# RWKV-7 beside sparse attention on one core: the first unit's finish, join and chain run as a stream beside the second unit's preparation, at rank offset 1000

## The chip, the cores and the metric

The kernel runs on one core of a Trainium2 chip. The metric is the device time of one execution in microseconds (us); the profile's times count from the start of the profiled execution.

## The reference: what is computed

One layer of a streaming encoder over 1024 new prompt frames and 32 frames of a running stream. One input projection feeds two head groups, whose outputs are concatenated, projected and followed by an MLP:

```
group A: indexer scores -> the top min(256, L // 4) keys of a query -> softmax attention over those keys
group B (RWKV-7), 8 heads of 64, a matrix state S per head, frame by frame:
    r, k, v, decay, a, g = projections of the token-shifted row
    S = S * diag(decay) + (S @ (-kk)) (kk * a)^T + v k^T
    y = S @ r ; then a norm per head, a bonus term and the gate g
out = x + [attention, rwkv] @ w_out ;  out = out + relu(norm(out) @ w1)^2 @ w2
```

## The kernel before: how the work is staged and ordered

**Stages.** From 0 to about 450 us the kernel projects, scores and makes the masks of the chosen keys. From there to 924 us two generators are interleaved by `body`: `attn_all` goes through the attention items (pairs of a key head and a tile of 128 queries), and `rwkv_all` through RWKV. The output projection follows (936 to 990), then the MLP (990 to 1802).

**An attention item** is `query` (transpose L1135, scalings L1138 on ACT and L1139 on DVE, which make the tile Q), `scores` (matmuls L1151 and L1152, masked on DVE at L1154, exponential on ACT at L1157), `turn` (transposes L1175, copied out at L1176) and `product` (matmuls L1191, transpose L1195, then L1197 to L1199). The masks themselves (`mb`) are finished on DVE and ACT at L387 to L405; the last of them are still being made when the first items run.

**RWKV** works in five units: four of 256 prompt frames, each in four chunks of 64, and one of 32 sample frames. The chunk form solves a triangular system per chunk, with these pieces:

- `rwkv_front` prepares a unit: low-rank projections L629, statistics L793, scans L650, broadcast L809, the tile KB at L684, and per chunk the matrix G (matmuls L715, masked at L718). It ends with the first part of `lane_inverse`, mostly on POOL.
- `finish` (the inner function of `lane_inverse`): 64 matmuls L856 (128 records in the trace), DVE L857, 64 matmuls L862, DVE L866 (4) and the transposes L871 (2).
- `rwkv_join`: matmuls L771, copies L774 on ACT, matmuls L779, copies L782.
- `rwkv_tokens`: transposes L749 and L753 for one chunk.
- `rwkv_back`, the chain, for each chunk: R (L906, and L910 with the state `st`), U (L918, copied out at L919 and L920), the new state S (L925) and the output Y (L936, L940). Each needs the one before, and the state goes from chunk to chunk and unit to unit.
- `rwkv_norm`: L978 to L1003.

**What sets the order.** The program is written out by the generators; then a scheduler gives each engine one fixed list by the ranks of the instructions. `S.tc.high_priority(n)` ranks what is written inside it n instructions earlier. The chain has BOFF = 300, the front of unit 0 F0 = 200, all others 0. Each engine then runs its list strictly in order. For the steps around the change `rwkv_all` (L1012 to L1077) decides: in its pass `i` it takes turns between the chain of unit `i`, the norm of unit `i - 1` and the front of unit `i + 2`. In pass -1, beside the front of unit 1, the generator `first` writes unit 0's tokens for two chunks, waits JOIN0 = 4 turns, writes `finish`, waits two turns and writes the join; unit 0's chain is begun in pass 0. For the later units `rwkv_back` itself writes the next unit's `finish` and join behind its own chunks. KB of unit 1 lies in the same memory as the last masks' working tile, so L684 of unit 1 waits for the mask work.

Of the kernel before, what the change touches and what calls it, by code (L numbers as in the profile page):

```python
# [79 lines left out]
def keys_of(t):  # L80
    return 128 * (t + 1) if t < 8 else 544
# [70 lines left out]
def phase_a(S, pwx, pwy, pa, pi, px, xp, ps, late):  # L152
# [102 lines left out]

    def key_T(A, B, col, src, r):
        pt = ps.tile([128, 512], F32, name="pt", bufs=2)
        nc.tensor.transpose(pt[:, :r], flat(src), S.ident[:r, :r])
        nc.scalar.copy(A[:, col:col + r], pt[:, :r])
        nc.vector.tensor_tensor(B[:, col:col + r], pt[:, :r], A[:, col:col + r].bitcast(F32), op=ALU.subtract)  # L260

# [40 lines left out]
    def idx_tile(t, W):  # L302
# [14 lines left out]
        n = keys_of(t)  # L317
        A, B = (ksA, ksB) if t == 8 else (kiA, kiB)
        for h in range(8):
            w = iw[:r, t, h:h + 1]  # L320
            rl = late["pj"].tile([128, 1024], F32, name="rl", bufs=2)
            for c0 in range(0, n, 512):
# [3 lines left out]
                nc.tensor.matmul(o, qs[:, h // 2, h % 2, :r], A[:, c0:c1], start=True, stop=False)  # L326
                nc.tensor.matmul(o, qs[:, h // 2, h % 2, :r], B[:, c0:c1], start=False, stop=True)
                nc.scalar.activation(rl[:r, c0:c1], o, AF.Relu)
# [269 lines left out]

def rwkv_front(S, u, U, B):

# [74 lines left out]
    yield  # L675
    while B and B.tokens < B.NC:
        yield
# [50 lines left out]
def rwkv_prelude(S, rp, U):  # L728
    nc = S.nc
    n, t0 = U.n, U.t0  # L730
    U.v = v = rp.tile([128, 4, 256], F32, name="v", bufs=2)[:, :, :n]
    nc.sync.dma_start(v, S.zsd[1024:1536, t0:t0 + n].rearrange("(h p) t -> p h t", p=128))
    U.zg = zg = rp.tile([96, 256], F32, name="zg", bufs=2)
    nc.sync.dma_start(zg[:, :n], S.zsd[1600:1696, t0:t0 + n])
    nc.scalar.activation(zg[:, :n], zg[:, :n], AF.Tanh, scale=0.5)
    nc.vector.tensor_scalar(zg[:, :n], zg[:, :n], 0.5, 0.5, op0=ALU.mult, op1=ALU.add)


def rwkv_tokens(S, rp, ps, U, c):

    nc, w = S.nc, U.w
    KBs = rp.tile([128, 2, 4, 64], F32, name="KBs", bufs=TOKB)
    VU = rp.tile([128, 2, 4, 64], F32, name="VU", bufs=TOKB)
    if w < 64:
        nc.gpsimd.memset(VU, 0.0)
    for par in range(2):
        p = ps.tile([128, 4, 64], F32, name=TOKP[0], bufs=TOKP[1])
        for hp in range(4):
            nc.tensor.transpose(p[:, hp], U.KB[PAR[par], c, hp].rearrange("p a b -> p (a b)"), S.ident[PAR[par], PAR[par]])  # L749
        nc.scalar.copy(KBs[:, par], p)  # L750
    p = ps.tile([64, 4, 2, 64], F32, name=TOKP[0], bufs=TOKP[1])
    for hp in range(4):
        nc.tensor.transpose(p[:w, hp].rearrange("p a b -> p (a b)"), U.v[:, hp, c * w:c * w + w], S.ident)  # L753
    for par in range(2):
        nc.scalar.copy(VU[par * 64:par * 64 + w, par], p[:w, :, par])
    U.tokens = c + 1
    return KBs, VU


def rwkv_join(S, ps, U):  # L760

    nc = S.nc
    X1 = U.X1.rearrange("p (c h) t -> p c h t", c=4)

    def pc():
        return ps.tile([128, 512], F32, name="pr", bufs=PRB).rearrange("p (a b c) -> p a b c", a=4, b=4)
    p = pc()
    for cc in range(4):
        for hp in range(4):
            for par, b in ((0, 64), (1, 0)):  # L770
                nc.tensor.matmul(p[b + 32:b + 64, cc, hp], U.G[b:b + 32, par, cc, hp, 32:64], X1[b:b + 32, cc, hp],  # L771
                                 start=True, stop=True)
    for par, b in ((0, 64), (1, 0)):
        nc.scalar.copy(X1[b + 32:b + 64], p[b + 32:b + 64])  # L774
    p = pc()
    for cc in range(4):
        for hp in range(4):
            for par, b in ((0, 64), (1, 0)):
                nc.tensor.matmul(p[b:b + 32, cc, hp], X1[b + 32:b + 64, cc, hp], U.G[b + 32:b + 64, par, cc, hp, 32:64],  # L779
                                 start=True, stop=True)  # L780
    for par, b in ((0, 64), (1, 0)):
        nc.scalar.copy(U.G[b:b + 32, par, :, :, 32:64], p[b:b + 32])  # L782
# [190 lines left out]
def rwkv_norm(S, rp, ps, U):  # L973

    nc = S.nc
    n, y = U.n, U.y
    for g, p in head_bcast(S, ps, U.bst, n):
        nc.vector.tensor_tensor(U.v[:, 2 * g:2 * g + 2], U.v[:, 2 * g:2 * g + 2], p, op=ALU.mult)  # L978
    yf = y.rearrange("p h c t -> p h (c t)")[:, :, :n]
    sq = S.rs.tile([128, 4, 256], F32, name="tmp", bufs=2)[:, :, :n]  # L980
    for g in range(2):
        p = ps.tile([128, 2, 256], F32, name="pr", bufs=PRB)[:, :, :n]
        for h in range(2):
            nc.tensor.matmul(p[:, h], S.cen, yf[:, 2 * g + h], start=True, stop=True)
        nc.scalar.activation(sq[:, 2 * g:2 * g + 2], p, AF.Square)
        nc.vector.tensor_copy(yf[:, 2 * g:2 * g + 2], p)
    yield
    rn = head_stat(S, ps, sq, n)
    nc.vector.tensor_scalar(rn, rn, 1.0 / 64, 64e-5, op0=ALU.mult, op1=ALU.add)
    rsqrt_small(S, rn, rn, rn.shape[1])  # L990
    yield
    for g, p in head_bcast(S, ps, rn, n):
        for h in range(2):
            hp = 2 * g + h
            nc.vector.scalar_tensor_tensor(yf[:, hp], yf[:, hp], S.pv[:, 64 + hp:65 + hp], p[:, h], op0=ALU.mult, op1=ALU.mult)
            nc.vector.scalar_tensor_tensor(yf[:, hp], yf[:, hp], S.pv[:, 68 + hp:69 + hp], U.v[:, hp], op0=ALU.add, op1=ALU.add)
    yield
    for g in range(2):
        p = ps.tile([128, 2, 256], F32, name="pr", bufs=PRB)[:, :, :n]
        for h in range(2):  # L1000
            hp = 2 * g + h
            nc.tensor.matmul(p[:, h], S.g2[:, hp * 128:hp * 128 + 128], U.zg[:, :n], start=True, stop=True)
        nc.vector.tensor_tensor(yf[:, 2 * g:2 * g + 2], yf[:, 2 * g:2 * g + 2], p, op=ALU.mult)  # L1003
    nc.sync.dma_start(S.od[512:1024, U.t0:U.t0 + n].rearrange("(h p) t -> p h t", p=128), yf)
    yield


YB = 2
JOIN0 = 4


def rwkv_all(S, order):  # L1012

    state = {"st": None}
    S.units = units = [K() for _ in order]
    fronts = []
    for i, U in enumerate(units):
        U.i, U.stage, U.tok = i, 0, []
        U.next = units[i + 1] if i + 1 < len(units) else None
        fronts.append(rwkv_front(S, order[i], U, units[i - 2] if i > 1 else None))  # L1020

    def ahead(i):

        for _ in fronts[i]:
            if units[i].stage == 2 and i + 1 < len(order) and PRE and i >= PREI:
                break
            yield
        else:
            return
        yield  # L1030
        for _ in range(PRE):
            next(fronts[i + 1])
            yield
        yield from fronts[i]

    def norm(i):
        if i >= 0:
            yield from rwkv_norm(S, S.P[0], S.ps, units[i])
        if 0 <= i + 2 < len(order):
            rwkv_prelude(S, S.P[0], units[i + 2])  # L1040

    def first():

        U = units[0]
        for c in range(2):
            U.tok.append(rwkv_tokens(S, S.P[0], S.ps, U, c))
            yield
        for _ in range(JOIN0):
            yield
        U.finish()  # L1050
        for _ in range(2):
            yield
        rwkv_join(S, S.ps, U)
        yield

    for i in range(-2, len(order) + 1):
        gens = []
        B = front = None
        if 0 <= i < len(order):
            B = units[i]  # L1060
            gens.append(back := rwkv_back(S, S.P[0], S.ps, B, state))
        if i >= -1:
            gens.append(norm(i - 1))
            if i == -1:
                gens.append(first())
            if i == 0:
                shift_rows(S, S.P[0], S.ps)
        if i + 2 < len(order):
            gens.append(front := ahead(i + 2))
        while gens:  # L1070
            for g in list(gens):
                with S.tc.high_priority(BOFF) if B and g is back else S.tc.high_priority(F0 if i == -2 else F1 if i == -1 else FOFF) if g is front else nullcontext():
                    if next(g, 1) == 1:
                        gens.remove(g)
                yield
# [338 lines left out]
F0 = 200  # L1414
F1 = 0
# [15 lines left out]
BOFF = 300  # L1431
TOKB = 3
FOFF = 0
# [156 lines left out]
```

## Time and profile before

| | us |
|---|---|
| runs of the kernel | 1806.84, 1811.15, 1806.84 (median 1806.84) |
| the profiled execution, time / span | 1804.16 / 1802.4 |
| PE busy in the span | 1683.8 (93%) |
| DVE, ACT, POOL busy | 915.8, 711.5, 530.5 |
| stretch 485 to 593 us: PE busy | 88.31 of 108 |
| stretch 593 to 924 us: PE busy | 313.71 of 331 |

The span is what the profiler's records cover; 1.76 us of the execution lie outside it. [...]

### The profile page before, as it was taken

To read this page: it belongs to the slowest core of one execution; us is meant where nothing else is said; L and a number is where in the kernel's file an instruction comes from. 1 tells how busy PE (TensorE), PEld (TensorE's weight loads), DVE (VectorE), ACT (ScalarE), POOL (GpSimd) and SP (SyncE) were. 2 spreads that over 40 slices of the span, in tenths; PEclk is the share of its full clock that TensorE was granted. 3 is DMA by queue.
4 is the path that set the end of the run, shared out by engine and by line. 5 is a ranking of instruction groups with operands and counts; after the bars stand their busy time and mean duration, and the time that the engine had idled before them with its cause. 6 is when DMAs were issued, how large, how long until landed. Compare 5 with 4: busy or idle time off the path is not lost.

```text
span 1802.4 us, 32468 instructions
## 1 busy us (share of the span) xinstructions
PE 1683.8 (93%) x12966; PEld 1525.7 (85%) x12966; DVE 915.8 (51%) x2016; ACT 711.5 (39%) x1559; POOL 530.5 (29%) x759
## 2 busy tenths in 40 slices
PE   7999979986688998999989999999999999999999
PEld 6787769986465877777668789999999999999998
DVE  6476899975876686664552632222222222222224
ACT  5365667897544453443631332222212121212120
POOL 6568863353312131122120022222212222222120
PEclk9999989996686797996989999999999999999999
DMA  7211131323100102020333341111111111111105
GB/s 213 58 35 43 42 87 61 111 70 87 32 27 18 38 21 59 25 96 15 90 91 108 123 125 47 47 48 36 53 41 53 41 51 44 47 40 55 36 17 170
DMA packets 161087, 112.77 MB, mean 63 GB/s; under 512 B 31632, under 2 KB 150120, under 8 KB 160936
## 3 DMA queue, kind: packets, MB, share of 16 engines
q1 hardware_dynamic: 152104, 106.37, 20.2%
q10 hardware_dynamic: 8832, 4.33, 0.9%
q8 instruction: 102, 1.67, 0.4%
q14 instruction: 49, 0.40, 0.1%
HBM read 85.65 MB, written 25.01 MB: 61 GB/s over the span
## 4 chain that ended last, share of the span: by engine, by line
PE 51%; DMA 1%; ACT 1%; DVE 1%; issue 0%; SPq 0%; POOL 0%; DVEq 0%; ACTq 0%
PE pd L1372 20%; PE pr L1392 10%; PE pc L1392 5%; PE po L1392 5%; PE pd L1308 3%; PE pr L1308 2%; PE po L1191 1%; PE ptr L1175 0%; PE ptr L1406 0%; DMA of<-od 0%; PE ptr L145 0%; PE pc L925 0%; DMA w1r<-in_w_ff_dram 0%; PE pr L749 0%; ACT G L1274 0%
## 5 line engine op out<-in xcount | busy, mean ns | idle before, releaser
L1372 PE MATMUL pd<-hh,w1h 128*128 128x352 f32 x768 | 248.6, 324 | 2.3 <-issue 1.5
L1372 PE MATMUL pd<-hh,w1l 128*128 128x352 f32 x768 | 248.2, 323 | 0.7 <-DVE w1l L1239 0.7
L1372 PE MATMUL pd<-hl,w1h 128*128 128x352 f32 x768 | 247.5, 322 | 0.0
L1378 DVE TENSOR_TENSOR h2l<-rl,h2h 128x352 fp32r<-128x352 f32 x96 | 56.8, 592 | 277.7 <-ACT h2h L1377 277.7
L1238 ACT CAST w2h<-w2r 128x512 fp32r<-128x512 f32 x64 | 39.8, 621 | 293.3 <-PE po L1392 144.7
L1376 POOL TENSOR_TENSOR rl<-rl 128x352 f32<-128x352 f32 x96 | 85.2, 888 | 215.6 <-ACT rl L1375 215.6
L1372 PEld LDWEIGHTS pd<-hh,w1h 128*128 128x128 f32 x768 | 144.7, 188 | 2.8 <-issue 1.7
L1372 PEld LDWEIGHTS pd<-hh,w1l 128*128 128x128 f32 x768 | 144.8, 189 | 0.9 <-DVE w1l L1239 0.9
L1372 PEld LDWEIGHTS pd<-hl,w1h 128*128 128x128 f32 x768 | 145.3, 189 | 0.0
L1239 POOL TENSOR_TENSOR w2l<-w2r,w2h 128x512 fp32r<-128x512 f32 x32 | 41.6, 1299 | 299.2 <-ACT w2h L1238 288.7
L1392 PE MATMUL pr<-h2h,w2l 128*128 128x352 f32 x384 | 124.3, 324 | 0.0
L1392 PE MATMUL pr<-h2h,w2h 128*128 128x352 f32 x384 | 124.3, 324 | 0.0
L1392 PE MATMUL pr<-h2l,w2h 128*128 128x352 f32 x384 | 124.2, 323 | 0.0
L363 ACT ACTIVATE AR<-G,cnd 128x768 bf16<-128x768 f32 (+2 forms) x93 | 96.8, 1041 | 42.8 <-DVE cnd L368 35.2
L1375 ACT ACTIVATE rl<-pd 128x352 f32<-128x352 f32 x96 | 44.3, 463 | 143.5 <-PE pd L1372 137.0
L1398 DVE TENSOR_TENSOR ya<-ya,pr 128x352 f32<-128x352 f32 x84 | 43.8, 521 | 100.7 <-PE pr L1392 100.7
L1175 PE MATMUL ptr<-ident,s 128*128 128x128 f32 (+2 forms) x328 | 67.8, 309 | 21.1 <-DVE Kl L1120 13.2
L1157 ACT ACTIVATE s<-s,m 32x544 f32<-32x544 f32 (+8 forms) x72 | 55.5, 771 | 64.1 <-DVE m L1154 62.4
L1377 ACT CAST h2h<-rl 128x352 fp32r<-128x352 f32 x96 | 46.6, 485 | 75.7 <-POOL rl L1376 75.7
L1392 PEld LDWEIGHTS pr<-h2l,w2h 128*128 128x128 f32 x384 | 72.3, 188 | 0.1
L1392 PEld LDWEIGHTS pr<-h2h,w2h 128*128 128x128 f32 x384 | 72.2, 188 | 0.1
L1392 PEld LDWEIGHTS pr<-h2h,w2l 128*128 128x128 f32 x384 | 72.3, 188 | 0.1
(452 smaller groups left out, 4593.3 us busy)
## 6 DMA issues: line engine op xcount, KB each, us to landing
w1r<-in_w_ff_dram SPq DMA_DIRECT2D x32, 512.0 KB, 4.2
w2r<-in_w_ff_dram SPq DMA_DIRECT2D x64, 256.0 KB, 2.7
zsd<-zm SPq DMA_DIRECT2D x12, 528.0 KB, 2.8
wraw<-in_w_in_dram SPq DMA_DIRECT2D x24, 256.0 KB, 2.7
wraw<-in_w_in_dram SPq DMA_DIRECT2D x40, 128.0 KB, 2.7
x<-in_x_prompt_dram SPq DMA_DIRECT2D x8, 512.0 KB, 4.3
hres<-hd ACTq DMA_DIRECT2D x16, 256.0 KB, 3.2
out_dram<-hres SPq DMA_DIRECT2D x16, 256.0 KB, 2.6
```

The source lines that it names most:

```text
L363: nc.scalar.activation(junk2[:r, :n], S.sc[t][:r, :n], AF.Sign, bias=c_of(j, r), scale=-1.0, accum_out=cnt[:r, j:j + 1])
L1157: nc.scalar.activation(s, s, AF.Exp, bias=m[:, i:i + 1], scale=-1.0, accum_out=w.m[:, 6 + h:7 + h])
L1175: nc.tensor.transpose(p[:x, i, h, :r], w.s[h][:, c0 + i * 128:c0 + i * 128 + x], S.ident[:r, :r])
L1239: (nc.vector if i % 2 else nc.gpsimd).tensor_tensor(lo, raw, hi.bitcast(F32), op=ALU.subtract)
L1308: nc.tensor.matmul(acc[:r], a[:, k], b, start=(i == 0), stop=(i == 23))
L1372: nc.tensor.matmul(acc, a[:, k], m[:, k, o:o + n], start=(i == 0), stop=(i == 23))
L1375: nc.scalar.activation(rl, acc, AF.Relu)
L1376: nc.gpsimd.tensor_tensor(rl, rl, rl, op=ALU.mult)
L1377: nc.scalar.copy(h2h[:, o:o + n], rl)
L1378: nc.vector.tensor_tensor(h2l[:, o:o + n], rl, h2h[:, o:o + n].bitcast(F32), op=ALU.subtract)
L1392: nc.tensor.matmul(acc, a[:, k], m[:, o:o + n], start=(i == 0), stop=(i == 11))
L1398: nc.vector.tensor_tensor(y, y, acc, op=ALU.add)
```

## The change

`JOIN0` goes and `JOFF` = 1000 comes. `first` now writes unit 0's tokens, its `finish` at once, the join after one turn, and then, as soon as unit 1's front is through, goes on into unit 0's chain as the same generator. All that it writes up to the join ranks 1000 instructions earlier; the chain behind it has 300, as before. Pass -1 ends when the front ends, and the stream runs on into pass 0. In every pass the norm now has its turn before the chain.

```diff
@@ first()
-        for _ in range(JOIN0):
-            yield
         U.finish()
-        for _ in range(2):
-            yield
+        yield
         rwkv_join(S, S.ps, U)
         yield
+        U.begun = True
+        while not hasattr(units[1], "finish"):
+            yield
+        yield from rwkv_back(S, S.P[0], S.ps, U, state)
+
+    back = first()
@@ the passes
-        if 0 <= i < len(order):
-            B = units[i]
-            gens.append(back := rwkv_back(S, S.P[0], S.ps, B, state))
+        if i > 0:
+            back = rwkv_back(S, S.P[0], S.ps, units[i], state) if i < len(order) else None
         if i >= -1:
             gens.append(norm(i - 1))
-            if i == -1:
-                gens.append(first())
+            if back:
+                B = units[max(i, 0)]
+                gens.append(back)
@@
-        while gens:
+        while [g for g in gens if i >= 0 or g is not back]:
             for g in list(gens):
-                with S.tc.high_priority(BOFF) if B and g is back else ...
+                with S.tc.high_priority(BOFF if hasattr(units[0], "begun") else JOFF) if B and g is back else ...
```

No instruction is added or removed; the change is one of order. In the changed kernel the lines behind L1006 are numbered two higher (L1151 is L1153 there). Three places show it.

PE behind the second attention item's last product (485 us in the trace); in the kernel before, the third item's query and scores follow at once:

```order
L1191 MATMUL po<-ph,vp 64x128 x2
L1195 MATMUL po<-ident,x 128x128
L1175 MATMUL ptr<-ident,s 128x128
L1135 MATMUL ptr<-ident,q 64x128 x2
L1175 MATMUL ptr<-ident,s 128x128 x3
L1151 MATMUL pd<-K,Q 128x384
L1152 MATMUL pd<-Kl,Q 128x384
```

and in the changed kernel:

```order
L1193 MATMUL po<-ph,vp 64x128 x2
L1197 MATMUL po<-ident,x 128x128
L856 MATMUL pr<-L,G 32x32 x64
L1177 MATMUL ptr<-ident,s 128x128 x4
L1137 MATMUL ptr<-ident,q 64x128 x2
L862 MATMUL pr<-Yl,L 32x32 x64
L1153 MATMUL pd<-K,Q 128x384
L1154 MATMUL pd<-Kl,Q 128x384
```

Unit 0's `finish` (L856, L862) has come here from behind unit 1's third G. From this place on PE's list differs until the tokens of unit 0's third and fourth chunk (592.88 us in the trace), where it is the same again up to the third unit's `finish`. In between, unit 0's join and first two chunks of the chain come before the last G of unit 1 instead of behind it.

DVE at the same time, in the last masks' work (L399 to L404); before:

```order
L1198 TENSOR_TENSOR t_5397<-t_5397,po 128x128
L1139 SCALAR_TENSOR_TENSOR Q<-ptr,Q 64x256
L399 TENSOR_TENSOR need_125<-need_125,cnt_121 128x1
L403 SCALAR_TENSOR_TENSOR KB<-ones,KB 128x768
L400 TENSOR_SCALAR need_125<-need_125 128x1
L1154 ISA s,m<-pd,mb_74 128x384
```

and in the changed kernel:

```order
L1200 TENSOR_TENSOR t_5605<-t_5605,po 128x128
L857 TENSOR_TENSOR L<-pr,lm 128x512
L399 TENSOR_TENSOR need_125<-need_125,cnt_121 128x1
L403 SCALAR_TENSOR_TENSOR KB<-ones,KB 128x768
L400 TENSOR_SCALAR need_125<-need_125 128x1
L399 TENSOR_TENSOR need_125<-need_125,cnt_121 128x1
L403 SCALAR_TENSOR_TENSOR KB<-ones,KB 128x896
L404 SCALAR_TENSOR_TENSOR KB<-KB,need_125,G 128x768
L400 TENSOR_SCALAR need_125<-need_125 128x1
L1141 SCALAR_TENSOR_TENSOR Q<-ptr,Q 64x256
L404 SCALAR_TENSOR_TENSOR KB<-KB,need_125,G 128x896
L866 TENSOR_TENSOR G<-pr,Yl 32x16x32 x4
```

The `finish` steps L857 and L866 stand among the mask work, and the third item's Q (L1141) behind two scans (L403) instead of ahead of them.

PE at the third unit's `finish` (685 us in the trace), where the second unit's chain is under way; before, single matmuls of `finish` (L856, tiles of 32 x 32) take turns with those of R (L906, then L910, tiles of 64 x 64), 15 of them in a row:

```order
L936 MATMUL pr<-G,VU 64x64 x8
L940 MATMUL pr<-AR,st 64x64 x8
L906 MATMUL pc<-VU,G 64x64
L856 MATMUL pr<-L,G 32x32
L906 MATMUL pc<-VU,G 64x64
L856 MATMUL pr<-L,G 32x32
```

and in the changed kernel:

```order
L906 MATMUL pc<-VU,G 64x64
L940 MATMUL pr<-AR,st 64x64
L910 MATMUL pc<-st,AR 64x64 x2
L856 MATMUL pr<-L,G 32x32
L910 MATMUL pc<-st,AR 64x64
L856 MATMUL pr<-L,G 32x32
```

R (L906) now takes turns with the output Y (L940), and 6 singles of L856 are left here. Counted over PE's list, singles of L856 between matmuls of R go from 15 to 6 at the third unit, from 14 to 3 at the fourth and from 1 to 3 at the fifth: 30 before, 12 now. The four transposes L753 that took turns with R of unit 0's second chunk (573 to 576 us) no longer do.

## Rows read from the trace of the kernel before

**Rows 1.** The page: its span and section 1, busy time of each engine

```profile
span 1802.4 us, 32468 instructions
...
PE 1683.8 (93%) x12966; PEld 1525.7 (85%) x12966; DVE 915.8 (51%) x2016; ACT 711.5 (39%) x1559; POOL 530.5 (29%) x759
```

**Rows 2.** Busy time by stage; columns: stretch, its length, engines, granted clock, DMA

```profile
485.00:593.00 108.00, 88.31 (x1266) 66.17 (x1266) 74.16 (x165) 52.46 (x117) 18.44 (x46) 0.77 0.09 24
593.00:924.00 331.00, 313.71 (x4093) 247.49 (x4093) 211.34 (x537) 153.96 (x387) 68.56 (x146) 0.87 0.16 47
...
990.00:1802.00 812.00, 804.88 (x4951) 791.26 (x4949) 243.05 (x411) 177.48 (x325) 166.93 (x152) 1.00 0.21 60
```

**Rows 3.** The same view of three pieces of 485 to 593 us

```profile
489.00:508.00 19.00, 10.72 (x48) 6.67 (x48) 18.29 (x32) 11.21 (x25) 0.55 (x3) 0.61 0.07 17
508.00:540.00 32.00, 31.65 (x460) 25.70 (x460) 23.19 (x66) 14.89 (x33) 4.09 (x5) 0.91 0.10 32
540.00:593.00 53.00, 44.30 (x751) 32.61 (x751) 32.29 (x68) 22.36 (x49) 13.50 (x38) 0.74 0.09 22
```

**Rows 4.** PE's waits from 485 to 593 us: in total, times, longest

```profile
PE pd L1151 <- DVE Q L1139: 4.9, 2, 2.9
```

**Rows 5.** DVE's timeline, 482 to 541 us: start, duration, instruction, wait before it

```profile
497.49 2.29 DVE L403 TENSOR_TENSOR_SCAN KB<-ones,KB 128x1024 f32<-128x1024 f32 x1
...
502.81 1.22 DVE L684 TENSOR_TENSOR KB<-k,D 64x1024 f32<-64x1024 f32 x1 [0.18 <-ACT mb L405]
...
528.09 0.69 DVE L857 TENSOR_TENSOR L<-pr,lm 128x512 f32<-128x512 f32 x1 [1.01 <-PE pr L856]
...
534.69 2.82 DVE L866 TENSOR_TENSOR G<-pr,Yl 32x512 f32<-32x512 f32 x4
537.54 0.70 DVE L871 STREAM_TRANSPOSE X<-G 32x512 f32<-32x512 f32 x1
```

**Rows 6.** PE's timeline, 508 to 576 us

```profile
508.24 0.80 PE L1151 MATMUL pd<-K,Q 128*128 128x512 f32 x1 [2.02 <-DVE Q L1139]
...
526.75 1.29 PE L856 MATMUL pr<-L,G 32*32 32x32 f32 x128
...
531.92 0.92 PE L862 MATMUL pr<-Yl,L 32*32 32x32 f32 x84
...
542.37 1.20 PE L771 MATMUL pr<-X,G 32*32 32x32 f32 x64
...
560.55 1.11 PE L918 MATMUL pc<-rh,G 64*64 64x64 f32 x14
...
573.43 0.42 PE L753 MATMUL pr<-ident,v 128*64 128x128 f32 x1
```

**Rows 7.** Busy time and granted clock, pieces of 4 us

```profile
544.00:548.00 4.00, 1.47 (x13) 1.09 (x14) 3.92 (x8) 0.00 (x0) 0.00 (x0) 0.99 0.06 16
548.00:552.00 4.00, 3.11 (x14) 1.53 (x13) 1.34 (x4) 2.87 (x5) 2.94 (x12) 0.50 0.01 2
...
692.00:696.00 4.00, 4.00 (x124) 3.38 (x122) 0.81 (x2) 0.00 (x0) 0.00 (x0) 0.50 0.00 0
```

**Rows 8.** PE's timeline at the third and the fifth unit's finish

```profile
685.99 0.28 PE L940 MATMUL pr<-AR,st 64*64 64x64 f32 x3
686.05 0.22 PE L906 MATMUL pc<-VU,G 64*64 64x64 f32 x1
686.06 0.28 PE L940 MATMUL pr<-AR,st 64*64 64x64 f32 x3
686.26 0.24 PE L856 MATMUL pr<-L,G 32*32 32x32 f32 x2
...
686.69 0.24 PE L856 MATMUL pr<-L,G 32*32 32x32 f32 x2
...
693.35 1.17 PE L856 MATMUL pr<-L,G 32*32 32x32 f32 x68
...
868.77 0.79 PE L856 MATMUL pr<-L,G 32*32 32x32 f32 x68
```

More of the change, by code (lines that the diff above doesn't have):

```diff
@@ L1008 @@
 YB = 2
-JOIN0 = 4
+JOFF = 1000
 def rwkv_all(S, order):
@@ L1069, in rwkv_all @@
             gens.append(front := ahead(i + 2))
-        while gens:
+        while [g for g in gens if i >= 0 or g is not back]:
             for g in list(gens):
-                with S.tc.high_priority(BOFF) if B and g is back else S.tc.high_priority(F0 if i == -2 else F1 if i == -1 else FOFF) if g is front else nullcontext():
+                with S.tc.high_priority(BOFF if hasattr(units[0], "begun") else JOFF) if B and g is back else S.tc.high_priority(F0 if i == -2 else F1 if i == -1 else FOFF) if g is front else nullcontext():
                     if next(g, 1) == 1:
```

## Prediction

> **What bounds the kernel now.** I read the page first [rows 1]: PE is busy for 1683.8 of 1802.4 us, DVE for half of them, so time comes out only where PE idles, runs at the lower clock, or does something inefficiently. The stages [rows 2] say where that can be: the MLP has PE busy for 804.88 of 812 us at clock 1.00 and holds none of the moved steps. The change touches 485 to 593 us, where PE is busy for 88.31 of 108 at clock 0.77, and, more weakly, 593 to 924, where it is busy for 313.71 of 331 at 0.87: the second stretch is full, but slowly run.
>
> The first stretch falls into three [rows 3], and the reader should see three different bounds. From 489 to 508 DVE is the bound: 18.29 of 19 us busy with the last masks (one scan is 2.29 us), and then with KB of unit 1 [rows 5], while PE has only 10.72. There PE's longest waits are for the items' scaled queries, 4.9 us in two waits [rows 4], and once more at 508.24, 2.02 us [rows 6]. From 508 to 540 PE is full, 31.65 of 32. From 540 to 593 nothing is full: PE 44.30, DVE 32.29 of 53, clock 0.74. This is the serial join and chain of unit 0 between few attention matmuls.
>
> **The change part by part.** No instruction comes or goes, so each term is a place that a step leaves or enters.
>
> (a) Unit 0's `finish` enters the mask stretch. Its steps on DVE take 0.69 (L857), 2.82 (L866, four) and two times 0.70 (L871): 4.9 us [rows 5]. DVE has 0.71 us free there [rows 3], so they push all behind them. The order puts the third item's Q behind two scans as well; walking DVE's new list with the old durations, Q of the item whose scores begin at 508.24 is ready some 6 us later. That takes 1.1 us for this reordering on top of the 4.9. **+6**. Behind it KB of unit 1 comes later by the same amount, and with it G, for which POOL's inverse of unit 1 waits. On SP the queries' loads move up with the order by one or two places in a queue that PE's waits don't name; I cost that, and POOL's copies that change places, at nothing, under cover of the DVE work; if it were gone, a late copy would cost its own wait, under 1 us.
>
> (b) The matmuls of that `finish` leave the full stretch: L856's 128 records are 1.29 us, L862's some 1.7 (84 of 128 records in 0.92, with two more pieces) [rows 6]. PE idles for 8.3 of 19 us where they go [rows 3], so they are hidden there. **-3**.
>
> (c) The join (64 records 1.20 us at full clock, twice) and U, S and R of the first chunks (five groups of 16, about 0.7 each, an estimate from 14 records in 1.11 at half clock [rows 6]) move from the loose stretch into the full one. At full clock they add 2.4 + 3.5, about 6 us; where they stood, part of it at clock 0.50, they took about 7. **-1** if the old place closes up behind them. Bounds: the loose stretch has 53 - 44.30 = 8.7 us of idle time and at clock 0.74 about half of its length at the lower level, so if all this vanishes the window wins up to 12 more; if nothing closes up, the 6 us stay as a loss.
>
> (d) The four transposes L753 that took turns with R (0.42 each [rows 6]) no longer do: at the price of a pair worked out in (e), **-1.4**. The window's sum is +6 - 3 - 1 - 1.4, about **+0.6**.
>
> (e) Later, singles of L856 take turns with matmuls of R in 12 places instead of 30. From one L856 to the next a pair takes 686.69 - 686.26 = 0.43 us; the same four records inside their own groups take about 4 x 0.0116 = 0.05 (868.77: 68 records in 0.79) and for R's two somewhat more, 0.09 in all [rows 8]. So a pair costs 0.34 too much, and 18 x 0.34 = **-6.1**. The new neighbours of R are Y's L940, 8 pairs at this place. In the trace of before such pairs start 0.01 us apart (686.05 and 686.06) [rows 8], and I take them at nothing. [...]
>
> (f) After that alternation the clock falls: in 692 to 696 it is 0.50 though PE is busy all the time [rows 7], and L856's 68 records take 1.17 us rather than 0.79 [rows 8]. Such a drop follows the alternation at two of the units. With shorter alternation it may go; between 0 and -4.9, the half-rate excess of both places, I take **-1.5**, since the third unit keeps 6 singles. Together (e) and (f) give -7.6, between -4.4 (a third of the pairs hidden behind other waits, clock unchanged) and -11.
>
> **Sum:** +0.6 - 7.6 = -7.0. The profiled execution took 1804.16 us, 2.7 below the median of the runs shown, 1806.84. So 1797.2 for a profiled execution, **1800** for the median. No change is within 0.3%, 5.4 us, which is about what a measurement of this kernel can tell: 1801.4 to 1812.3.
>
> **The rivals.**
>
> *Slower, about 1814.* DVE is the bound of the mask stretch and the 6 us of (a) are never caught up. PE then runs out of work near 510, where G of unit 1 and the next item's scores both wait for DVE, for about 4 us. In the trace a thin stretch of that kind is followed by the lower clock: PE busy for 1.47 of 4 us from 544, then clock 0.50 [rows 7]. The same behind 510 would run the matmuls of the full stretch at half rate for 10 us, +5. The window would lose 11, downstream gain 4.4: +6.6, 1813.4. The point at which it decides is a loss of 10 us in the window. For it: rows 3 and 4. Against: rows 6, a wait of 2.02 us at 508.24, behind which the clock of the stretch is still 0.91 on average. [...] Chance 0.21.
>
> *No change, about 1806.* The list of PE is the same again from 592.88 us on, so the chain may end its second chunk when it did, or the window loses 5 to 7 us, which is what is gained later. For it: the attention items, not the chain, fill PE up to the end of the stage; against: the pairs of (e) are seen in PE's own time. That the change lasts in nothing is the same case. Chance 0.27.
>
> *Much faster, about 1787.* The loose stretch closes up: of 8.7 us of idle and some 15 lost to the lower clock 12 go, and downstream gives 7.6. For it: the chain is what was serial there. Against: unit 1's preparation comes later by (a), and its inverse then ends the stretch. Chance 0.13.
>
> **How the numbers follow.** The forecast, 1793 to 1801.4 within its own bounds, has 0.39; with the last rival that makes faster 0.52, no change 0.27, slower 0.21. For 8 in 10 the range must take in the case of no change and the lower part of the slower one, and half of the fastest: 1789 to 1813. The lower end is the forecast with a window gain of 10 (+0.6 becomes -10, less than the bound of 12), the upper the slower rival's.
>
> **What the profile will show.** Right: DVE full from 489 to 514 or so and the PE wait behind it longer than 2.02 us; PE's first L856 near 485; between 540 and 600 less idle than 8.7 us; at the third unit's `finish` about 8 pairs fewer and no 0.50 behind it; the MLP's length unchanged. Wrong: the MLP beginning at the same time while the pairs are gone (then another wait took their place), a clock below 0.8 from 510 to 540 (the slower rival), or a new wait of PE for POOL's inverse of unit 1, at its `finish` near 583 us.

## The result: 1.2% faster, from a window that the forecast took as even

| | median of the runs, us | lowest to highest | profiled execution, time / span |
|---|---|---|---|
| before | 1806.84 | 1803.69 to 1811.15 (4) | 1804.16 / 1802.4 |
| changed | 1785.46 | 1782.01 to 1786.34 (4) | 1782.01 / 1780.2 |

The ratio is 0.9877, with an interval of 0.9852 to 0.9901. The forecast was 1800 with a range of 1789 to 1813: the sign is right, the time lies below the range, at the rival called "much faster, about 1787".

The page of the changed kernel, its head (answers to [rows 1]):

```profile
span 1780.2 us, 32465 instructions
## 1 busy us (share of the span) xinstructions
PE 1667.3 (94%) x12966; PEld 1514.6 (85%) x12966; DVE 913.7 (51%) x2016; ACT 711.4 (40%) x1559; POOL 533.1 (30%) x759
```

PE is busy for 16.5 us less with the same instructions. Where, the busy time by stretches shows. I cut both traces at the same instructions: the end of the second attention item, of the sixth, the tokens of unit 0's third chunk (from there PE's list is the same again), the U of unit 2's second chunk and the first matmul of the output projection. Columns as in [rows 2]; first the kernel before:

```profile
484.90:523.40 38.50, 27.52 (x163) 20.59 (x161) 30.10 (x76) 26.21 (x61) 4.64 (x7) 0.71 0.10 28
523.40:592.88 69.48, 60.78 (x1106) 45.56 (x1104) 43.95 (x90) 26.35 (x58) 13.79 (x39) 0.80 0.09 22
592.88:756.10 163.22, 156.34 (x1935) 126.61 (x1927) 107.27 (x273) 76.45 (x200) 26.07 (x55) 0.84 0.13 37
756.10:935.94 179.84, 162.60 (x2232) 125.09 (x2231) 108.31 (x279) 82.82 (x201) 44.11 (x92) 0.88 0.22 68
```

The changed kernel at the same instructions:

```profile
482.70:536.30 53.60, 39.42 (x573) 29.85 (x571) 36.62 (x86) 29.86 (x68) 4.71 (x8) 0.67 0.08 24
536.30:578.25 41.95, 37.86 (x696) 29.22 (x694) 36.31 (x80) 22.54 (x51) 15.51 (x38) 1.00 0.12 31
578.25:743.50 165.25, 161.10 (x1934) 131.07 (x1927) 107.31 (x272) 77.00 (x200) 26.29 (x55) 0.79 0.13 36
743.50:913.49 169.99, 153.50 (x2228) 118.62 (x2227) 107.67 (x278) 82.04 (x201) 44.24 (x92) 0.91 0.23 71
```

The first piece is 15.1 us longer, the second 27.5 shorter, the third 2.0 longer, the fourth 9.9 shorter. From the projection to the end both take between 866 and 867 us. The runs below include a second trace of each kernel; its four pieces are 39.9, 70.7, 163.8, 180.1 before and 53.7, 41.8, 165.8, 170.2 changed, so these differences come back.

What a piece is made of can be worked out from such rows taken for every microsecond: what PE is not busy is **idle**; busy time x (1 - granted clock) is what the **lower clock** costs (the granted clock of the rows is a share of full clock, 1.00; at 0.50 half of the busy time is counted); the rest is **work** at full clock. Mean of both traces of each kernel, changed minus before:

| piece | length | idle | lower clock | work |
|---|---|---|---|---|
| second to sixth item | +14.5 | +3.4 | +4.4 | +6.7 |
| to the tokens | -28.2 | -5.3 | -12.8 | -10.2 |
| to unit 2's second U | +2.0 | -2.7 | +8.7 | -4.0 |
| to the projection | -9.9 | -0.9 | -7.6 | -1.4 |
| sum | -21.6 | -5.5 | -7.3 | -8.9 |

The split takes all work to last twice as long at 0.50, which is not exact. At the third unit's `finish` in the kernel before, an alternating pair (L856, then R) takes 0.43 us at clock 1.00 and 0.64 at 0.50. And e1 below, which has the list of the kernel before from the tokens to unit 2's second U, shows there 2.7 us less work beside 20.3 us more of lower clock. So the columns are good to some 3 us.

In the mask stretch PE's longest waits (answers to [rows 4]) are these in the changed kernel, from 483 to 579 us:

```profile
PE ptr L1177 <- ACT s L1159: 8.4, 4, 5.4
PE pd L1153 <- DVE Q L1141: 3.5, 1, 3.5
PE pr L862 <- DVE L L857: 1.8, 1, 1.8
```

The new one, 5.4 us on ACT, is DVE's doing, as DVE's timeline of the changed kernel shows (answers to [rows 5]):

```profile
492.27 0.42 DVE L1141 SCALAR_TENSOR_TENSOR Q<-ptr,Q 64x256 fp32r<-64x256 f32 x1
492.72 1.15 DVE L404 SCALAR_TENSOR_TENSOR KB<-KB,need,G 128x896 f32<-128x896 f32 x1
493.90 2.82 DVE L866 TENSOR_TENSOR G<-pr,Yl 32x512 f32<-32x512 f32 x4
...
496.83 2.28 DVE L403 TENSOR_TENSOR_SCAN KB<-ones,KB 128x1024 f32<-128x1024 f32 x1
499.15 0.70 DVE L871 STREAM_TRANSPOSE X<-G 32x512 f32<-32x512 f32 x1
499.88 0.56 DVE L1156 CUSTOM_DVE_ANT_0 s<-pd,mb 128x384 f32<-128x384 f32 x1
```

The mask step L1156 of the third item's scores stands behind L404, L866, L403 and L871, while PE had those scores done at 494.4. ACT's exponential and PE's transposes wait for it.

The three pieces of [rows 3] in the changed kernel, the last one up to the tokens:

```profile
489.00:508.00 19.00, 9.48 (x60) 5.82 (x49) 17.99 (x29) 6.36 (x13) 0.29 (x1) 0.50 0.05 15
508.00:540.00 32.00, 29.19 (x313) 23.38 (x313) 18.59 (x60) 18.19 (x41) 4.13 (x6) 0.78 0.10 29
540.00:578.25 38.25, 34.16 (x654) 25.94 (x652) 33.75 (x75) 21.55 (x48) 15.51 (x38) 1.00 0.13 32
```

The clock of 508 to 540 fell from 0.91 to 0.78, as the slower rival had it; but the stretch behind, 53 us at 0.74 before, now takes 38 at 1.00.

At the third unit's `finish` the changed kernel's PE timeline reads (answers to [rows 8]):

```profile
677.83 0.22 PE L906 MATMUL pc<-VU,G 64*64 64x64 f32 x1
677.83 0.22 PE L940 MATMUL pr<-AR,st 64*64 64x64 f32 x1
677.84 0.22 PE L906 MATMUL pc<-VU,G 64*64 64x64 f32 x1
677.85 0.22 PE L940 MATMUL pr<-AR,st 64*64 64x64 f32 x1
...
678.11 0.24 PE L856 MATMUL pr<-L,G 32*32 32x32 f32 x2
...
678.53 0.24 PE L856 MATMUL pr<-L,G 32*32 32x32 f32 x2
```

R beside Y, both in tiles of 64 x 64, advances by some 0.03 us a pair (16 pairs begin between 677.37 and 677.85); R beside L856, in tiles of 32 x 32, still by 0.42, from 678.11 to 678.53. What makes the second kind of pair dearer is not shown.

### The profile page after: what moved, and what is told of

Read it like the earlier page. It is cut to its first block, busy times and chain, and to the rows that moved or that the text cites. A ratio compares the mean times of both kernels' runs of the same rounds, so it can differ in the third digit from the quotient of the medians.

```text
span 1780.2 us, 32465 instructions
## 1 busy us (share of the span) xinstructions
PE 1667.3 (94%) x12966; PEld 1514.6 (85%) x12966; DVE 913.7 (51%) x2016; ACT 711.4 (40%) x1559; POOL 533.1 (30%) x759
## 4 chain that ended last, share of the span: by engine, by line
PE 50%; DMA 2%; ACT 1%; DVE 1%; issue 1%; SPq 0%; POOL 0%; ACTq 0%; DVEq 0%; POOLq 0%
PE pd L1374 20%; PE pr L1394 10%; PE pc L1394 5%; PE po L1394 5%; PE pd L1310 3%; PE pr L1310 2%; DMA of<-od 1%; PE po L1193 1%; DMA w1r<-in_w_ff_dram 0%; PE ptr L1177 0%; PE ptr L1408 0%; PE pc L925 0%; PE pd L1153 0%; PE ptr L145 0%; ACT G L1276 0%
## 5 line engine op out<-in xcount | busy, mean ns | idle before, releaser
L1380 DVE TENSOR_TENSOR h2l<-rl,h2h 128x352 fp32r<-128x352 f32 x96 | 56.8, 592 | 276.7 <-ACT h2h L1379 276.7
L1177 PE MATMUL ptr<-ident,s 128*128 128x128 f32 (+2 forms) x328 | 66.3, 304 | 18.7 <-ACT s L1159 9.5
```

Source lines behind the costliest of these rows:

```text
L1177: nc.tensor.transpose(p[:x, i, h, :r], w.s[h][:, c0 + i * 128:c0 + i * 128 + x], S.ident[:r, :r])
L1380: nc.vector.tensor_tensor(h2l[:, o:o + n], rl, h2h[:, o:o + n].bitcast(F32), op=ALU.subtract)
```

## The experiments

Fourteen runs beside the kernel before, which had medians of 1804 to 1807 in them; twelve were executed 4 to 10 times, e7 and e8 once. The table has each run's median, its ratio to the kernel before with an interval, and what its trace from 450 us to 700 us ahead of its end is made of, worked out as above. A trace shows one execution: the lower clock's cost differs by 2.8 us between the two traces of the kernel before and by 4.3 between those of the changed one, and the executions traced of e1 and e9 lie 5.0 and 10.5 us above their medians.

| run | edit against | median | ratio (interval) | idle | lower clock | work |
|---|---|---|---|---|---|---|
| before, two traces | | 1806.84 | | 59.6, 61.1 | 76.2, 79.0 | 516.6, 513.0 |
| changed, two traces | before | 1785.46 | 0.9877 (0.9852 to 0.9901) | 55.7, 54.2 | 67.7, 72.0 | 506.7, 507.7 |
| e1_window | before | 1807.18 | 0.9997 (0.9973 to 1.0021) | 61.4 | 91.4 | 507.6 |
| e2_tail | changed | 1791.7 | 0.9932 (0.9909 to 0.9955) | 67.6 | 68.6 | 507.4 |
| e3_join_late | changed | 1810.58 | 1.0034 (1.0010 to 1.0057) | 52.1 | 95.3 | 509.7 |
| e4_chain_late | changed | 1793.36 | 0.9941 (0.9920 to 0.9961) | 63.0 | 66.0 | 512.7 |
| e5_after_nopairs | changed | 1788.92 | 0.9897 (0.9865 to 0.9928) | 57.2 | 69.8 | 504.4 |
| e6_before_nopairs | before | 1798.44 | 0.9937 (0.9910 to 0.9965) | 53.5 | 85.5 | 507.7 |
| e9_finish_one_turn | changed | 1807.85 | 1.0012 (0.9981 to 1.0042) | 61.6 | 107.6 | 497.4 |
| e10_finish_three_turns | changed | 1789.57 | 0.9901 (0.9870 to 0.9932) | 68.4 | 62.0 | 505.6 |
| e11_join_block | changed | 1791.32 | 0.9905 (0.9876 to 0.9933) | 56.3 | 78.5 | 503.3 |
| e12_rank0 | changed | 1799.24 | 0.9971 (0.9942 to 0.9999) | 50.5 | 91.7 | 504.8 |
| e13_fill | changed | 1793.72 | 0.9918 (0.9881 to 0.9955) | 58.0 | 69.4 | 513.6 |
| e14_before_fill | before | 1821.83 | 1.0084 (1.0058 to 1.0110) | 56.7 | 92.0 | 518.8 |

### Is it the window or what follows? e1 and e2

e1, the window's order without the stream (the waiting turns keep the later passes near their old phase):

```diff
-        for _ in range(JOIN0):
-            yield
         U.finish()
-        for _ in range(2):
-            yield
+        yield
         rwkv_join(S, S.ps, U)
-        yield
+        for _ in range(6):
+            yield
...
-                gens.append(first())
+                gens.append(fst := first())
...
+                with S.tc.high_priority(1000) if g is fst else ...
```

> The kernel before, with finish written at once, the join after one turn, both at rank offset 1000, and six waiting turns behind, so that the passes keep about their old phase. PE's list is the changed kernel's up to the third unit's finish; behind it the third unit's finish is as before, and 30 singles of L856 take turns with R (14 in the changed kernel by this count). Theory A (the pairs cost 0.34 us each, the window gave 14.6): about 1792, some 6 above the changed kernel, and nearly all of that 6 at the later units' finishes. Theory B (what came off later is not the pairs but the earlier chain that shifts everything): 1785, like the changed kernel. Theory C (the window's gain belongs to the one stream): 1800 or more.

e2, the stream with the window's old order:

```diff
-JOFF = 1000
+JOFF = 0
...
+        for _ in range(4):
+            yield
         U.finish()
-        yield
+        for _ in range(2):
+            yield
         rwkv_join(S, S.ps, U)
```

> The changed kernel with the four turns before finish, the two before the join and rank offset 0 put back: PE's list is that of the kernel before up to the third unit's finish, behind which 14 singles of L856 are left instead of 30. Theory A: the window gives nothing, the pairs about 5 to 8 us: 1799 to 1802. Theory B: 1806, no change. Theory C (the stream itself gives the window's gain): 1792.

e1 came out even with the kernel before, 15 us above theory A; e2, at 1791.7, took 7 to 10 more off than theory A gives. Both times are those of theory C, but its mechanism is not in the traces: e1 has the window's gain without the stream, and in e2, with the stream, the same matmuls from the second item to the tokens take 104.3 us, much nearer to the kernel before (108.0 and 110.6) than to the changed one (95.6 and 95.5). The trace of e1 tells where its window's gain went: the tokens begin at 578.88, 14.0 us earlier than before, as in the changed kernel. Behind them PE's list is that of the kernel before, word for word, up to behind unit 2's second chunk, and yet it takes longer. First e1, from the tokens to the U of that chunk, and a piece of it:

```profile
578.88:756.80 177.92, 174.12 (x1937) 141.16 (x1929) 107.47 (x272) 77.27 (x201) 26.29 (x55) 0.74 0.12 34
706.30:742.70 36.40, 36.40 (x356) 29.65 (x355) 12.93 (x40) 14.28 (x42) 2.76 (x5) 0.52 0.10 29
```

and the same piece in the kernel before:

```profile
713.90:742.10 28.20, 28.07 (x358) 23.06 (x357) 12.89 (x40) 14.02 (x43) 2.77 (x5) 0.73 0.12 37
```

The same matmuls take 36.4 us instead of 28.2, at clock 0.52 instead of 0.73, with PE busy in every microsecond. From the tokens to unit 2's second U it is 177.9 instead of 163.2 us: in this execution the 14 us of the window are given back to the clock. That this can happen is theory F of the later runs (where the lower clock falls decides the gain). The trace is of the slowest of e1's ten executions; four of the ten lie near 1799.

e1 also has a loss of its own: PE waits 9.4 us for DVE (L145 on L136) as the MLP begins, which neither kernel does. e2, e4, e9 and e10 have the same wait, 9.5 us. What it costs can be estimated from the stretch between 880 and 780 us ahead of the end: PE does 82.2 us of work there in e1 and 84.6 to 85.4 in the other four, but 89.3 in both traces of the changed kernel. So some 4 to 7 us of the times of these five versions are this wait's, and a total alone does not tell what they did to the window.

### Which part of the window closes it? e3 and e4

e3:

```diff
         U.finish()
-        yield
+        U.begun = True
+        for _ in range(8):
+            yield
         rwkv_join(S, S.ps, U)
```

> The changed kernel with eight turns between finish and join, and the join at the chain's rank: finish stays early, on DVE among the last masks, while the join and unit 0's chain stand on PE about where they stood before; 31 singles of L856. Theory D (the loose stretch closes because 4.9 us of DVE work left it): the window keeps most of its gain, 1790 to 1795 in all. Theory E (it closes because the join and the chain start some 25 us earlier): the window's gain is lost and the 10 us that finish costs in the mask stretch stay: 1806 to 1815.

e4:

```diff
-    with S.tc.high_priority(BOFF if hasattr(units[0], "begun") else JOFF) if ...
+    with S.tc.high_priority((-150 if i < 1 else BOFF) if hasattr(units[0], "begun") else JOFF) if ...
```

> The changed kernel with unit 0's chain at rank offset -150: finish and join stay early, the chain's first U too, but U and S of its second and third chunk come 50 and 40 matmuls later on PE, 15 singles of L856. Theory D: 1785 to 1788, as changed. Theory E (the chain's own time is the bound): the chain's steps end at about their old places in the loose stretch, 5 to 10 us of the window's gain lost: 1790 to 1796.

Both times are theory E's, 1810.6 and 1793.4, but the traces don't bear E out. Take the 96 us behind the second item's end, which is the length of the changed kernel's window, in the kernel before, the changed kernel, e3 and e4:

```profile
484.90:580.90 96.00, 76.62 (x856) 56.42 (x854) 67.57 (x150) 48.74 (x108) 16.99 (x43) 0.75 0.07 20
482.70:578.70 96.00, 77.73 (x1271) 59.45 (x1270) 73.28 (x166) 52.39 (x118) 20.23 (x46) 0.81 0.10 27
482.90:578.90 96.00, 78.81 (x1255) 60.53 (x1253) 73.91 (x163) 50.44 (x112) 18.40 (x43) 0.80 0.08 21
484.90:580.90 96.00, 78.51 (x996) 59.56 (x994) 71.97 (x163) 49.73 (x112) 20.29 (x45) 0.80 0.07 20
```

Summed by microsecond, PE does 56.9 us of work in them in the kernel before (56.8 in its second trace), 64.8 in the changed one (64.4), 64.2 in e3 and 66.3 in e4. The instructions differ from version to version, so this compares work and not lists. Neither e3 nor e4 lost the window's gain, although in e3 the join begins at its old place (57.6 us behind the second item; 57.5 before, 42.5 changed), and in e4 the U of unit 0's last chunk comes at 114.8 (119.5 before, 107.1 changed). The loose stretch does not need the early join and chain to close.

What they lost lies elsewhere. e3's idle is lower than the changed kernel's, and all that it is behind it, 27 us, is lower clock. One stretch alone:

```profile
580.00:638.00 58.00, 58.00 (x506) 48.18 (x506) 25.06 (x73) 22.36 (x57) 5.59 (x9) 0.50 0.15 39
```

e4 has no more lower clock than the changed kernel. Against its first trace it has 7.3 us more idle and 6.0 more work; the idle lies behind the window, above all in the wait as the MLP begins:

```profile
PE ptr L145 <- DVE tmp L136: 9.5, 1, 9.5
```

### The pairs: e5, e6 and e11

e5 and e6, the same edit in either kernel:

```diff
-            U.next.finish()
+            with S.tc.high_priority(-100):
+                U.next.finish()
```

> The changed kernel with the later units' finish ranked 100 instructions later, so that it stands in one block behind R: no single of L856 between matmuls of R is left (14 before); the window's list is unchanged. Theory A (a pair costs 0.34 us): 14 x 0.34 = 4.8 less, 1780 to 1781; with the clock no longer falling behind the pairs down to 1777. Theory F (not the pairs but where the lower clock falls decides the later gain): within 1782 to 1790, with no relation to the pairs.

> The same rank for finish in the kernel before: the window's list is unchanged up to unit 1's finish, the 30 singles are gone. Theory A: 30 x 0.34 = 10.2 less, 1794 to 1797; with the clock's part down to 1792. Theory F: 1800 to 1808, no change that shows.

e11:

```diff
-            rwkv_join(S, ps, U.next)
+            with S.tc.high_priority(100):
+                rwkv_join(S, ps, U.next)
```

> The changed kernel with the later units' joins ranked 100 instructions earlier: the window's list is the same, and the 7 singles of L771 that take turns with S (L925) behind a wait of 3.5 us are gone. Theory A (pairs): 7 x 0.34 to 0.65, 2.4 to 4.5 less, 1781 to 1783. Theory F: the lower clock behind that wait (798 to 809) lasts otherwise, and the time moves by more than the pairs are worth, to either side: 1775 to 1795.

The work column moves as worked out, but by less in e5 and e6: 7.1 us less for e6 (mean of before 514.8; 10.2 expected), 2.8 less for e5 (4.8 expected), 3.9 less for e11 (2.4 to 4.5). Two traces of the kernel before differ by 3.6 in this column, and in e5 and e6 the 7 singles of L771 are gone as well, so the price of a pair is confirmed only roughly. In e5's trace L856's first 70 records of unit 2 stand together:

```profile
676.06 0.80 PE L856 MATMUL pr<-L,G 32*32 32x32 f32 x70
676.90 0.68 PE L918 MATMUL pc<-rh,G 64*64 64x64 f32 x16
```

The time follows the work only in e6, and there by less than expected. e5 is no faster than the changed kernel, and e11 is 5.9 us above it. In e11 the wait on ACT ahead of S stays, and the lower clock behind it lasts:

```profile
800.00:820.00 20.00, 18.22 (x203) 14.01 (x204) 6.17 (x17) 8.62 (x22) 9.10 (x32) 0.50 0.08 19
```

In the changed kernel that stretch ends at 809. Theory F predicted such a miss to either side, theory A did not; but F's range, 20 us wide, would have held nearly any outcome.

### Does the trace repeat? e7 and e8

> The kernel before once more, for a second trace: if the same list has the same clock, its stretches at 0.50 (545 to 562, 568 to 581, 596 to 616, 691 to 698, 709 to 729, 815 to 842) are there again, within 1 us; if the clock differs from execution to execution, some are missing or longer, and the time differs by their half.

> The changed kernel once more, for a second trace: if the window's full clock from 525 to 579 us belongs to its order, it is there again, and the tokens of unit 0's last chunks (L749) begin near 578 us; if it was a chance of the one execution, they begin up to 10 us later.

1804.89 and 1785.75 us. The second trace of before has the lower clock at 548 to 559, 569 to 586, 596 to 613, 688 to 702, 709 to 729 and 815 to 842: the same places, but their ends are up to 4 us apart and not within the 1 us expected. The second trace of the changed kernel has no lower clock from 529 to 583, and from its second item to its tokens it takes 95.5 us (95.6 in the first). So the window's gain belongs to the order and not to one execution.

### Finish behind the masks, and the rank: e9, e10, e12

e9 and e10, with 1 and 3 turns:

```diff
+        for _ in range(1):
+            yield
         U.finish()
```

> The changed kernel with one turn put ahead of finish: finish comes behind the last masks (on DVE behind KB of unit 1, on PE 97 matmuls later), the join 50 matmuls later, 14 singles of L856 as in the changed kernel, none of the join. Theory D (finish's DVE work costs the mask stretch 10 to 13 us, and the early join alone closes the loose stretch): the window shrinks by up to 10 more, 1775 to 1781. Theory F (how long the lower clock lasts behind it decides): what the window wins comes back as lower clock, 1782 to 1800.

> The same with three turns: finish 116 matmuls later than in the changed kernel and only 14 ahead of its old place, the join 66 later (42 ahead of its old place). Theory D: as with one turn or slightly less, 1777 to 1783. If the window's gain needs the early finish itself: 1790 to 1800. Theory F: 1782 to 1800, whatever the window does.

e12 sets JOFF = 0.

> The changed kernel with JOFF = 0: finish stands at the same place on PE's list, the join and the chain 12 to 19 matmuls earlier, since 30 of attention's fall behind; 14 singles of L856. If the place of finish and join is what counts and not the rank: 1782 to 1792. If the rank of 1000 is needed: 1800.

Theory D, which here means that the early join alone closes the loose stretch, fell: e9 took all that the change had won, more than theory F allowed too, and e10 lies at 1789.6. In the 96 us behind the second item PE does 59.2 us of work in e9 and 61.9 in e10, less than the changed kernel's 64.8. e9's trace has two long stretches as well:

```profile
589.00:651.00 62.00, 60.16 (x516) 48.71 (x514) 25.89 (x73) 23.17 (x60) 4.42 (x7) 0.50 0.10 28
715.00:763.00 48.00, 48.00 (x460) 39.58 (x459) 17.16 (x51) 18.61 (x57) 4.21 (x8) 0.50 0.14 38
```

110 us at clock 0.50, in the second 48 of 48 busy. e10 has the least lower clock of all, 62.0, but the most idle, 68.4, in part by the wait of 9.5 us as its MLP begins.

e12's 1799.2 is the time that was expected if the rank of 1000 is needed. With finish in its place, and the join and the chain 12 to 19 matmuls earlier, it lost 14 us, and not in the window: PE does 65.2 us of work in the 96 us. Its trace has 58 of 58 us busy at 0.50 from 577 to 635; in the changed kernel the clock comes back at 617.

Put together, the 96 us sort the traces by the place of unit 0's `finish`. Where its first matmuls come right behind the second item (changed, e1, e3, e4, e5, e11, e12), PE does 64.2 to 66.3 us of work; where they come 37 us or more later (before, e2, e6, e9, e10), 56.6 to 61.9. So the early `finish` is enough for the window's gain, wherever the join and the chain stand in these seven. Why it is enough is not separated: its DVE steps leave the loose stretch, and its result is ready earlier.

### Small tiles or waits? e13 and e14

The same edit in either kernel:

```diff
         p = pj()
+        for l in range(8):
+            nc.tensor.matmul(p[:, 4 * (l % 4):4 * (l % 4) + 4], S.cen, S.ident, start=True, stop=True)
         for l in range(16):
```

> The changed kernel with eight more matmuls of 128x128 on the whole array in each unit's finish, ahead of L862, written into the tile that L862 then overwrites, so that the result stays the same: 40 in all, at 0.165 us each (four L1175 in 0.66) 6.6 us of added work at full clock. Theory G (the lower clock falls behind stretches in which only 32x32 tiles are busy, and whole-array work among them shortens it): the lower clock between 485 us and the MLP costs some 10 us less than the 68 to 72 of the changed kernel's two traces, and the time is 1776 to 1785 in spite of the added work. Theory H (waits set the lower clock, not the kind of matmul): its cost stays, and the time is 1786 to 1796.

> The same eight matmuls in the finish of the kernel before. Theory G: the lower clock costs 10 us or more less than the 76 to 79 of its two traces, 1796 to 1804. Theory H: 1806 to 1814.

e13's work is 6.4 us more than the changed kernel's (6.6 expected) and its lower clock the same, 69.4. In e14 the lower clock costs more than before, 92.0. Theory G fell. That waits set the clock, theory H, is not shown by this: e13 is within H's range, e14 8 us above it, and the scheduler moved other work as well. e14 is also the one exception to the sorting above: its `finish` is late, 44.9 us behind the second item, and yet PE does 69.2 us of work in the 96 us (67.0 in e13, whose `finish` is early), of which up to 2.6 are added matmuls. So an early `finish` is not the only way to close the window. e13 has another 48 us like those of e9:

```profile
700.00:748.00 48.00, 48.00 (x435) 39.28 (x434) 17.48 (x52) 16.85 (x51) 3.54 (x7) 0.50 0.10 27
```

None of these versions beats the changed kernel.

## Why the prediction was wrong, step by step

**(a), +6 for finish in the mask stretch:** right in sign and mechanism, too small. Up to the sixth item the changed kernel is 14.5 us longer, of which 6.7 is work moved in (finish 3.0 and the join 2.4 by the forecast's own prices) and 7.8 is idle and lower clock. The forecast pushed the queries back but not the mask step of the scores, behind which ACT waits for 4.3 and PE for 5.4 us.

**(b) and (d)** are in the work column. (b) is a move from the window's second piece to its first, and is seen in both; over the window the work is 3.5 us less, of which (d) had forecast 1.4; where the rest comes from is not shown.

**(c), -1 "if the old place closes up behind them":** the step that failed. The loose stretch did more than take back the moved work; from the sixth item to the tokens the kernel is 28.2 us shorter: 10.2 work (6.7 of it only moved ahead), 12.8 lower clock and 5.3 idle. The forecast gave "up to 12 more" as its bound and chose nothing of it. The window's sum, +0.6 in the forecast, is 14.5 - 28.2 = -13.7. This is the rival "much faster", with its mechanism and nearly its number; its chance of 0.13 was too low, and "unit 1's preparation comes later", which spoke against it, did not end the stretch: unit 1's `finish` waited 0.4 us for its inverse. The forecast also tied the closing to the join and the chain, "what was serial there"; e3 closes the stretch with the join at its old place, and what the closing versions but e14 share is the early `finish`.

**(e), -6.1 for the pairs:** right as work: -5.4 behind the tokens. By the count in e1's expectation 14 singles are left and not 12, and 16 x 0.34 is 5.4. **(f), -1.5 for the clock there:** measured +1.1, made of +8.7 and -7.6, each larger than the term. "No 0.50 behind" the third unit's `finish` did not come: from 689 to 716 us the changed kernel is at 0.50 with PE busy for 26.7 of 27 us. With 3.6 us of idle this makes -7.9 behind the tokens where -7.6 was forecast: the right sum, but not by the right path. The clearest case is the join of unit 3 (the fourth unit), where before and after have nearly the same list:

```profile
808.30:841.42 33.12, 29.96 (x342) 22.39 (x341) 13.32 (x27) 10.87 (x27) 9.23 (x32) 0.59 0.12 40
```

in the kernel before, and in the changed one, from U to U,

```profile
793.10:820.28 27.18, 22.83 (x341) 17.26 (x341) 12.55 (x26) 10.66 (x27) 9.19 (x32) 0.81 0.07 17
```

The transposes L809 in it take 1.97 us in the first and 1.09 in the second:

```profile
839.52 1.97 PE L809 MATMUL pr<-ident,tmp 128*128 128x128 f32 x8
```

```profile
819.26 1.09 PE L809 MATMUL pr<-ident,tmp 128*128 128x128 f32 x8
```

5.9 of the 7.9 us lie there, at a place that the forecast did not name: the clock came back at 809 in the changed kernel and at 841 in the one before.

**The slower rival** happened in its first half (a wait of PE near 501 and 511, the clock of 508 to 540 at 0.78), and was then outdone. PE waits 2.65 us up to 510.89, and from 512 to 525 the clock is 0.50, with PE busy all the time. That the wait brings the clock down was the author's reading; the trace shows only that the one follows the other. In the stretches of 48 and 58 us at 0.50 PE was busy throughout, so idling inside them is not what kept the clock low.

**The method** failed in one point: the terms were added as if the clock of the rest stayed. e1 shows the failure: its tokens begin 14.0 us earlier, and the list behind them, the same as before, takes 14.7 us more. That the gains of parts don't add is not shown by the totals: e1 (the window) and e2 (the rest) are worth 0 and 12 us alone and 21 together, but both hold the wait as the MLP begins, and without it, by the estimate above, they would be worth some 7 and 17. Over all 16 traces the span goes with the lower clock's cost (correlation 0.83) and not with idle (0.01).

Open: why the early `finish` closes the loose stretch, and what lets PE fall to 0.50 and stay there while it is busy. Fewer pairs (lower clock of 69.8 us in e5, 85.5 in e6), added matmuls of 128 x 128 (69.4 in e13, 92.0 in e14) and a later finish (107.6 in e9, 62.0 in e10) did not lower its cost reliably.

## What to carry to other kernels

Price a reordering in three columns, idle, work and lower clock, each from its own rows; the work column could be forecast to some 3 us in e5, e6, e11 and e13 (though e4 and e9 moved by +5.5 and -9.8 that nobody had forecast), and the clock column moved by up to 40 for a single waiting turn (e9). Where the lower clock costs some 75 us of a stage (76.2 and 79.0 here, in the two traces of the kernel before), give a rival that closes the stretches at 0.50 more than a token chance, and don't credit a saved microsecond before the trace behind it is seen. And compare versions stretch by stretch: e3 and e4 lost 25 and 8 us in all and kept the whole gain of the window, so their totals alone point to the wrong cause.

## What the runs showed of the hardware that was not expected

PE stays at clock 0.50 for 48 to 58 us while it is busy without a gap (58 in e3 and e12, 48 in e9 and e13), and the same list of matmuls takes 28.2 us in the kernel before and 36.4 in e1; whether that comes from what ran ahead of it or from the execution is not separated. Executions of one kernel can differ by as much as the change is worth: 1790.43 to 1811.82 for e12, while the changed kernel's four runs lie within 4.3 us. And PE pauses inside L862's 128 small records for no wait that the profile names, twice in the changed kernel ahead of a fall of the clock:

```profile
577.16 1.16 PE L862 MATMUL pr<-Yl,L 32*32 32x32 f32 x113 [1.27 <-issue]
...
687.99 0.31 PE L862 MATMUL pr<-Yl,L 32*32 32x32 f32 x12 [1.62 <-issue]
```
